# Dense matmuls in runs of three, carried over block and unit ends, in a hybrid decoder layer

## The chip, the cores and the metric

The kernel runs on one core of one Trainium2 chip. The metric is the device time of one execution in microseconds (us); the median of several runs is compared. All of the layer's weights, about 280 MB in 32-bit floats, are read once from HBM in every execution.

## The reference

One decoder layer over 256 tokens of width 2048, and a last normalization:

```
h = rms_norm(x, ln1_w);  proj = h @ w_in              # 2048 -> 10792 columns
o_a = nsa_attention(...)                              # 8 heads of 128, from proj
o_b = gated_deltanet(...)                             # 8 heads of 128, from proj
g_a, g_b = split(sigmoid(merge), 2)                   # merge: last 4096 columns of proj
x = x + (g_a * (o_a @ w_pa) + g_b * (o_b @ w_pb)) @ w_o
h = rms_norm(x, ln2_w)
x = x + square(relu(h @ w_up)) @ w_down               # 2048 -> 8192 -> 2048
out = rms_norm(x, ln_f_w)
```

The attention and the delta rule are small here; nearly all of the work is the product of 256 tokens with the weight matrices.

## The kernel before

**Tiling.** The tokens stand in the columns and the features in the partitions. A *unit* is 128 output features with a contraction over 2048, so 128 x 2048 weights. It is worked in four *blocks* (q = 0 to 3), each with four 128x128 pieces of weights. Each 32-bit operand is split into a high part that TensorE takes in its fast 32-bit format, and the low rest. The split of weights gives `wh` and `wl` (tile `wt`), that of activations 256 columns of high parts with 256 columns of low parts behind them. The product is then wh x high, wh x low and wl x high. wh meets all 512 columns in one matmul; wl meets 256 columns in another. Both add into one PSUM tile `gp` of 512 columns (three such buffers), the first with high and low products side by side; the evacuation adds the halves.

**The order of a block.** `mm3` issues a block's four 512-column matmuls (line 247; an *H* below) and then its four 256-column ones (line 249; an *l*). An H and the l of the same weights are a *pair*, so a block is four pairs, HHHH llll. Each matmul loads its own 128x128 weights, and that load runs beside the matmul before it. The first units of the kernel, which need only 256 of the columns, go by `mm3n` instead: three 256-column matmuls for each piece of weights (lines 255 to 257).

**The list of units.** `seq` sets the order: the input projections with attention and delta-rule preparation between them; 32 merge units (two for each of 16 `dm`), of which the first two end at unit nM; 16 units that project the heads (`pu`, operand `osp`, each with two halves of two blocks); at unit nB, 16 units of the output projection (`wo`, operand `m`); at nB + 16 the first half of the MLP's up-projection (32 units, operand `xs2`, which the trace calls `xs`), at nB + 48 its down-projection (32 units, operands `hA` and `hB`), at nB + 80 and nB + 112 the same for the other half. The last two units go by `mm3n`.

**The loop.** One pass of the loop at the end of `build` is one block `b`. It issues weight loads on SyncE's queue, starts the evacuations of units that ended in the block before (`pend`), splits the weights of block b + 6 (`split_at(b + LOOK)`: one ScalarE copy, line 69, and one VectorE subtraction, line 108, into one of seven `wt` buffers), issues block b's matmuls, and lets each pending small task (`step_tasks`) go on by one step. These tasks issue the attention's and the delta rule's small matmuls, *side work* below, into PSUM tiles from `sideps`; so side work stands between blocks.

Of the kernel before, what the change touches and what calls it, by code (L numbers as in the profile page):

```python
# [26 lines left out]
T = 256  # L27
# [7 lines left out]
LOOK = 6  # L35
# [13 lines left out]
def build(tc, xt, lnv, vecs, rel, onehot, win, wsm, wc, wpab, wo, wup, wdn, out):  # L49
    nc = tc.nc  # L50
    ctx = ExitStack()
    V, S, G, PE = nc.vector, nc.scalar, nc.gpsimd, nc.tensor
# [5 lines left out]
    hold = ctx.enter_context(tc.tile_pool(name="hold", bufs=1))  # L58
    psum = ctx.enter_context(tc.tile_pool(name="psum", bufs=1, space=bass.MemoryType.PSUM))
    ctx.enter_context(tc.manual_schedule())  # L60

    def sideps(name="sp"):
        return psum.tile([128, 512], F32, name=name, tag="side", bufs=4)

    def gps(name="gp"):
# [10 lines left out]
    def load(u, q, n=2):  # L76

        un = units[u]
        w = un.cols // 4
        if q % 2 == 0:  # L80
            raws[u, q // 2] = stream.tile([128, 2 * w], F32, name="raw", tag="raw", bufs=NRAW)
        o = (q % 2) * w
        nc.sync.dma_start(out=raws[u, q // 2][:, o:o + n * w], in_=un.src[:, q * w:(q + n) * w])
# [3 lines left out]
    def split(b):  # L87
        u, q = blocks[b]
        w = units[u].cols // 4
        raw = raws[u, q // 2]  # L90
        if units[u].prep:
            whs[b], wls[b] = raw, None
            return
        raw = raw[:, (q % 2) * w:(q % 2) * w + w]
        wt = stream.tile([128, 2 * w], FR, name="wt", tag="wt", bufs=LOOK + 1)
        c = 40 if units[u] is sm else w
        r, p = raw.rearrange("p (k c) -> p k c", c=c), wt.rearrange("p (k a c) -> p k a c", a=2, c=c)
        whs[b], wls[b] = (wt, None) if c < w else (wt[:, :w], wt[:, w:])
        if c < w:
            act(p[:, :, 0], r, AF.Copy)  # L100
            V.tensor_tensor(p[:, :, 1], r, p[:, :, 0].bitcast(F32), op=OP.subtract)
            return
        wh, wl = whs[b], wls[b]
        n = 2 if b == 0 else 1
        for i in range(n):
            c = slice(i * w // n, (i + 1) * w // n)
            act(wh[:, c], raw[:, c], AF.Copy)
            V.tensor_tensor(wl[:, c], raw[:, c], wh[:, c].bitcast(F32), op=OP.subtract)  # L108
            if b == 0:
                x_split(2 * i, 2)  # L110
# [70 lines left out]
    def warm(n):  # L181

        w = sideps("warm")
        for i in range(n):
            PE.matmul(w[:, :T], zs[:, :128], zs, start=(i == 0), stop=(i == n - 1))
# [7 lines left out]
    def row_pow(ps, power):  # L193

        col = tmp.tile([128, 2], F32, name="rc", tag="rc", bufs=2)
        for c in range(2):
            V.tensor_scalar(col[:, c:c + 1], ps[c][:, 0:1], 1.0 / D, EPS, op0=OP.mult, op1=OP.add)
        if power == -0.5:
            G.tensor_tensor(col, col, mhalf, op=OP.pow)
            yield  # L200
        else:
            V.reciprocal(col, col)
        dg = tmp.tile([128, 2, 128], F32, name="dg", tag="dg", bufs=1)
        for c in range(2):
            V.tensor_scalar(dg[:, c], ident, col[:, c:c + 1], None, op0=OP.mult)
        yield
        bc = sideps()
        PE.matmul(bc[:, :T], ones, dg.rearrange("p c t -> p (c t)"), start=True, stop=True)
        return bc

    def row_stat(sq, dst, power):
        ps = [sideps() for _ in range(2)]
        row_sum(ps, sq, True, True)
        bc = yield from row_pow(ps, power)
        act(dst, bc[:, :T], AF.Copy)
# [4 lines left out]
    def spawn(gen):  # L220
        tasks.append(gen)

    def start(gen):
        tasks.append(gen)
        advance(gen)

    def advance(g):
        try:
            next(g)
        except StopIteration:  # L230
            tasks.remove(g)
# [5 lines left out]
    def step_tasks():  # L237
        cnt["step"] += 1
        for g in list(tasks):
            advance(g)  # L240


    def mm3(ps, wh, wl, rhs, M, first, last):


        for j, r in enumerate(rhs):
            PE.matmul(ps[:M, :], wh[:, j * M:(j + 1) * M], r, start=(first and j == 0), stop=False)  # L247
        for j, r in enumerate(rhs):
            PE.matmul(ps[:M, :T], wl[:, j * M:(j + 1) * M], r[:, :T], start=False, stop=(last and j == 3))  # L249
# [68 lines left out]


    gk, gv, gz, kc = {}, {}, {}, {}  # L320
    cnt = {"pc": 0, "at": 0, "step": 0, "last": -9, "lb": 0, "pool": 0, "heads": 0}
    done = set()

    def ev_gdn(h, which):
# [638 lines left out]
    nM = len(seq)  # L963
# [8 lines left out]
    nB = len(seq)  # L972
# [13 lines left out]
    while u < len(units):  # L986
        n = 2 if units[u].prep else 1
# [4 lines left out]
    def x_split(k, n):  # L992
        for k in range(k, k + n):
            act(xs[:, k, :T], xT[:, k, :], AF.Copy, scale=ln1[:, k:k + 1])
            V.scalar_tensor_tensor(xs[:, k, T:], xT[:, k, :], ln1[:, k:k + 1], xs[:, k, :T].bitcast(F32),  # L995
                                   op0=OP.mult, op1=OP.subtract)
# [39 lines left out]
    def split_at(b):  # L1036
        if b >= len(blocks):
            return
        split(b)
        if 0 < b < 4 * NI and b % NI == 0:  # L1040
            x_split(4 * (b // NI), 4)
        for f, *args in sqat.get(b, ()):
            f(*args)
# [5 lines left out]
    def stat1():  # L1049
        V.tensor_scalar(vec[:, VEC_CONV:VEC_CONV + 96], vec[:, VEC_CONV:VEC_CONV + 96], 0.5, None, op0=OP.mult)  # L1050
        yield from row_stat(sqs, R, -0.5)
        spawn(bias_table())
        done.add("R")


    pend = []
# [4 lines left out]
    at = {x: b for b, x in enumerate(blocks)}  # L1061
    lastq = [at[u, q + 1] + (LOOK if units[u].prep else 0) for u, q in halves if units[u] is not sm]
    halves = [x for x in halves if x[0] >= NI]
    for b, (u, q) in enumerate(blocks):
        if b == 4 * nM + 1:
            while not all(("gdn", h) in done for h in range(H)):
                step_tasks()
            pools["a1"].release()
            pp["th"] = tc.alloc_tile_pool(name="thp", bufs=1, side="right")
        if b == 4 * nA:  # L1070
            while tasks:
                step_tasks()
            pool_a2.release()
            pool_b = tc.alloc_tile_pool(name="pb", bufs=1)
            mt["m"] = pool_b.tile([128, KD, 2 * T], FR, name="m", tag="m32")
        if b == 4 * nB:
            mt["xs2"] = hold.tile([128, KD, 2 * T], FR, name="xs2", tag="xs")
        if b == 4 * (nB + 16):
            hB = pool_b.tile([128, KD, 2 * T], FR, name="hB", tag="m32")
            mt["h"] = [hold.tile([128, 2 * T], FR, name="hA", tag=f"o{k}") for k in range(KD)]  # L1080
            mt["h"] += [hB[:, k, :] for k in range(KD)]
        while loaded < len(halves) and lastq[max(0, loaded + 6 - NRAW)] < b + LOOK:
            load(*halves[loaded])
            loaded += 1
        if "R" in done:
            for f, ps in pend:
                start(f(ps))
            pend = []
        if b == 4 * nB:
            pp["th"].release()  # L1090
            pool_x = tc.alloc_tile_pool(name="px", bufs=1, side="right")
            mt["x"] = pool_x.tile([128, KD, T], F32, name="x2")
            for c in range(4):
                nc.gpsimd.dma_start(out=mt["x"][:, 4 * c:4 * c + 4, :], in_=xt[:, 4 * c:4 * c + 4, :])
        split_at(b + LOOK)
        for n in (12, 20):
            if b + n < len(blocks):
                un = units[blocks[b + n][0]]
                if un.prep and blocks[b + n][1] == 0 and (un is cu[0, 0]) == (n == 20):
                    spawn(un.prep())  # L1100
        un = units[u]
        ps = un.gemm(q, whs.pop(b), wls.pop(b))
        if b == 4 * NI:
            pool_x0.release()
            pools["a1"] = tc.alloc_tile_pool(name="pa1", bufs=1)
            spawn(stat1())
        if q in un.evac:
            pend.append((un.evac[q], ps))
        clock += 0.44 if un.prep else 1.3
        if clock >= 1.2:  # L1110
            clock = 0.0
            step_tasks()
# [9 lines left out]
    y = pool_b.tile([128, 2, D], F32, name="y", tag="m32")  # L1122
# [85 lines left out]
```

## Time and profile before

| what | value |
|---|---|
| median of 3 runs | 1493.62 us (1493.16 to 1494.17) |
| profiled execution, its own time | 1492.99 us |
| span of that execution, first to last instruction | 1491.2 us |
| TensorE (PE) busy | 99% of the span, 9578 matmuls recorded |
| VectorE (DVE), ScalarE (ACT), GpSimd (POOL) busy | 70%, 55%, 17% |
| DMA | 285 MB, 191 GB/s |
| chain of work that ended last | 89% on PE, 47% on line 247, 24% on line 249 |

The span is read as one long row of matmuls with some holes. Since a matmul's record overlaps the next one's, its duration says little; what a matmul costs is the distance from its start to the start of the next one. That is called its *step* here. The timeline view merges equal matmuls that follow each other, gives the start of the first and how many there are, and so gives the steps of a run by the difference of two rows.

### The profile page before, as it was taken

What the parts mean: (1) busy time and instruction counts of PE and PEld (TensorE: products, weight loads), DVE (VectorE), ACT (ScalarE), POOL (GpSimd) and SP (SyncE); (2) the same over time, 40 slices, a digit from 0 to 9 for tenths busy, and PEclk for the clock granted to TensorE, in tenths of its full rate; (3) what the DMA queues carried; (4) which work ended last, traced back from release to release, by engine and by line L of the source; (5) the groups of instructions that cost most, each with busy time, mean ns of one, the idle gap of its engine ahead of it and who ended that gap; (6) DMA issues with size and microseconds to landing.
All of it is one profiled execution on the core that took longest, in us unless ns stands there. A gap on an engine that the chain in (4) does not pass through costs nothing.

```text
span 1491.2 us, 26400 instructions
## 1 busy us (share of the span) xinstructions
PE 1475.2 (99%) x9578; PEld 1319.6 (88%) x9578; DVE 1038.1 (70%) x2062; ACT 814.9 (55%) x1738; POOL 259.3 (17%) x615
## 2 busy tenths in 40 slices
PE   8999999999999999999999999999999999999997
PEld 7999998889988888888888888888888888888887
DVE  7877777656787677787986776665566767766664
ACT  6655565545565555565655555544445555555553
POOL 1066788742000000002320000000000000011211
PEclk9999999999999999999999999999999999999999
DMA  8466666786444555556655555555555555555552
GB/s 288 156 194 192 191 209 191 221 264 230 146 143 158 180 192 188 192 190 222 215 188 192 188 194 188 193 188 194 188 186 195 190 191 190 192 189 191 188 193 75
DMA packets 86446, 285.33 MB, mean 191 GB/s; under 512 B 13187, under 2 KB 14723, under 8 KB 86316
## 3 DMA queue, kind: packets, MB, share of 16 engines
q1 hardware_dynamic: 85596, 281.52, 57.9%
q0 software_dynamic: 576, 2.10, 0.4%
q8 instruction: 75, 1.23, 0.3%
q14 instruction: 55, 0.45, 0.1%
q10 hardware_dynamic: 144, 0.02, 0.0%
HBM read 279.20 MB, written 4.41 MB: 190 GB/s over the span
## 4 chain that ended last, share of the span: by engine, by line
PE 89%; issue 3%; POOL 2%; DVE 2%; DMA 2%; ACT 1%; SPq 0%; POOLq 0%; DVEq 0%; ACTq 0%
PE gp L247 47%; PE gp L249 24%; PE gp L255 5%; PE gp L256 4%; PE gp L257 4%; DMA raw<-in_win_dram 1%; DMA ldr<-lq 1%; POOL ft L492 1%; PE cps L644 1%; POOL tb L494 1%; ACT wt L69 1%; PE pAo L788 0%; DVE wt L108 0%; PE pPT L777 0%; PE pK L453 0%
## 5 line engine op out<-in xcount | busy, mean ns | idle before, releaser
L108 DVE TENSOR_TENSOR wt<-raw,wt 128x512 fp32r<-128x512 f32 (+1 forms) x977 | 682.9, 706 | 328.7 <-ACT wt L69 322.4
L69 ACT ACTIVATE wt<-raw 128x512 fp32r<-128x512 f32 (+1 forms) x977 | 604.0, 625 | 301.9 <-PE gp L249 159.2
L247 PE MATMUL gp<-xs,wt 128*128 128x512 f32 x1536 | 419.5, 395 | 0.0
L247 PEld LDWEIGHTS gp<-xs,wt 128*128 128x128 f32 x1536 | 261.2, 188 | 33.4
L249 PEld LDWEIGHTS gp<-xs,wt 128*128 128x128 f32 x1536 | 232.8, 188 | 32.3
L255 PE MATMUL gp<-xs,wt 128*128 128x256 f32 x832 | 244.7, 294 | 1.5 <-ACT xs L69 0.9
L249 PE MATMUL gp<-xs,wt 128*128 128x256 f32 x1536 | 239.7, 278 | 0.0
L257 PE MATMUL gp<-xs,wt 128*128 128x256 f32 x832 | 232.7, 280 | 0.3 <-DVE wt L108 0.2
L256 PE MATMUL gp<-xs,wt 128*128 128x256 f32 x832 | 232.8, 280 | 0.1
L255 PEld LDWEIGHTS gp<-xs,wt 128*128 128x128 f32 x832 | 156.6, 188 | 11.4 <-issue 5.8
L256 PEld LDWEIGHTS gp<-xs,wt 128*128 128x128 f32 x832 | 156.8, 188 | 1.1 <-DVE xs L995 0.7
L257 PEld LDWEIGHTS gp<-xs,wt 128*128 128x128 f32 x832 | 156.3, 188 | 1.1 <-DVE wt L108 1.1
L247 PE MATMUL gp<-hA,wt 128*128 128x512 f32 x496 | 134.4, 393 | 0.0
L247 PE MATMUL gp<-hB,wt 128*128 128x512 f32 x496 | 134.4, 393 | 0.0
L69 ACT ACTIVATE a<-gp 128x256 f32<-128x256 f32 x175 | 67.1, 383 | 105.8 <-PE gp L249 105.6
L290 DVE TENSOR_TENSOR t<-gp,a 128x256 f32<-128x256 f32 x159 | 67.5, 425 | 56.1 <-ACT a L69 56.0
L918 POOL TENSOR_TENSOR sqs<-x 128x256 f32<-128x256 f32 x1 | 0.9, 906 | 541.8 <-DVE x L905 541.8
L494 POOL TENSOR_TENSOR tb<-tb,ft 128x62 f32<-128x62 f32 (+30 forms) x248 | 90.4, 365 | 19.4
L247 PEld LDWEIGHTS gp<-hB,wt 128*128 128x128 f32 x496 | 84.2, 188 | 10.6
L247 PEld LDWEIGHTS gp<-hA,wt 128*128 128x128 f32 x496 | 84.2, 188 | 10.7
L249 PEld LDWEIGHTS gp<-hA,wt 128*128 128x128 f32 x496 | 75.2, 188 | 10.4
L249 PEld LDWEIGHTS gp<-hB,wt 128*128 128x128 f32 x496 | 75.2, 188 | 10.4
(278 smaller groups left out, 1555.4 us busy)
## 6 DMA issues: line engine op xcount, KB each, us to landing
raw<-in_win_dram SPq DMA_DIRECT2D x162, 512.0 KB, 4.4
raw<-in_wup_dram SPq DMA_DIRECT2D x128, 512.0 KB, 4.4
raw<-in_wdn_dram SPq DMA_DIRECT2D x128, 512.0 KB, 4.4
raw<-in_wpab_dram SPq DMA_DIRECT2D x32, 512.0 KB, 4.4
raw<-in_wo_dram SPq DMA_DIRECT2D x32, 512.0 KB, 4.2
raw<-in_wc_dram SPq DMA_DIRECT2D x16, 512.0 KB, 5.7
lb<-ldr SPq DMA_DIRECT2D x32, 128.0 KB, 5.2
raw<-in_win_dram SPq DMA_DIRECT2D x11, 256.0 KB, 7.8
```

Source lines behind the costliest of these rows:

```text
L69: return S.activation(o, i, f, **kw)
L108: V.tensor_tensor(wl[:, c], raw[:, c], wh[:, c].bitcast(F32), op=OP.subtract)
L247: PE.matmul(ps[:M, :], wh[:, j * M:(j + 1) * M], r, start=(first and j == 0), stop=False)
L249: PE.matmul(ps[:M, :T], wl[:, j * M:(j + 1) * M], r[:, :T], start=False, stop=(last and j == 3))
L255: PE.matmul(ps[:M, :T], w, r[:, :T], start=(first and j == 0), stop=False)
L256: PE.matmul(ps[:M, :T], w, r[:, T:], start=False, stop=False)
L257: PE.matmul(ps[:M, :T], wl[:, j * M:(j + 1) * M], r[:, :T], start=False, stop=(last and j == 3))
L290: V.tensor_tensor(t[:M], ps[:M, :T], a[:M], op=OP.add)
L492: G.tensor_tensor(ft[:, :, :w], tb[:, :, j:j + 1].to_broadcast([128, 2, w]), lbs[j // 16][:, j - o, :, j - o + 1:], op=OP.mult)
L494: G.tensor_tensor(tb[:, :, j + 1:], tb[:, :, j + 1:], ft[:, :, :w], op=OP.subtract)
L644: PE.matmul(ps[32 * j:32 * j + 32, :256], sf[:, 2 * q - 2 + j, :], wh[:, 256 * j:256 * j + 256], start=(u == 0 and q == 1), stop=(u == 3 a ...
L918: G.tensor_tensor(sqs, x2, x2, op=OP.mult)
```

## The change

From the merge units' third one on (block 4 nM), `mm3` keeps the l matmuls in a list, `run["lo"]`, and issues them after every third H (`run["need"]`), whatever block or unit these H belong to. So the order is HHH lll, and a run goes over block and unit ends. After side work (a counter in `sideps` tells of it) the next run counts four H; l that were kept before the side work are issued with it, five or six in a row. At the units in `ends` (nB, nB + 16, nB + 48, nB + 80, nB + 112 and the last two) the kept l are issued at the end of the block, and the next run has four H.

```diff
+    run = {"on": False, "side": 0, "n": 0, "need": 3, "lo": []}
+
+    def run_flush(need):
+        for p, M, w, r, stop in run["lo"]:
+            PE.matmul(p[:M, :T], w, r[:, :T], start=False, stop=stop)
+        run.update(n=0, need=need, lo=[])
...
     def mm3(ps, wh, wl, rhs, M, first, last):
+        if run["on"]:
+            if run["side"] != cnt["side"]:
+                run.update(side=cnt["side"], n=0, need=4)
+            for j, r in enumerate(rhs):
+                PE.matmul(ps[:M, :], wh[:, j * M:(j + 1) * M], r, start=(first and j == 0), stop=False)
+                run["lo"].append((ps, M, wl[:, j * M:(j + 1) * M], r, last and j == 3))
+                run["n"] += 1
+                if run["n"] == run["need"]:
+                    run_flush(3)
+            return
...
+    ends = [4 * x - 1 for x in (nB, nB + 16, nB + 48, nB + 80, nB + 112, nB + 142, nB + 144)]
     for b, (u, q) in enumerate(blocks):
+        if b == 4 * nM:
+            run["on"] = True
...
         if "R" in done:
+            late = [x for x in pend if any(x[1] is y[0] for y in run["lo"])]
             for f, ps in pend:
-                start(f(ps))
-            pend = []
+                if not any(ps is y[1] for y in late):
+                    start(f(ps))
+            pend = late
...
-        split_at(b + LOOK)
+        if not run["on"]:
+            split_at(b + LOOK)
...
         ps = un.gemm(q, whs.pop(b), wls.pop(b))
+        if b in ends:
+            run_flush(4)
+        if run["on"]:
+            split_at(b + LOOK)
```

Two things come with it. A unit whose last l are still kept has its evacuation started one block later (`late`). And the split of block b + 6 is issued behind block b's matmuls, since the `wt` buffer that it takes is that of block b - 1, whose last l may stand among them.

The matmuls' number and operands stay as they were: 3040 pairs by `mm3` in both programs. The three places that matter follow, on PE's queue; line 261 is where the changed `mm3` issues an H, and line 249 is by chance an l in both.

The first place is the last side work of the attention (`pAo`) among the merge and head projections. Before:

```order
L247 MATMUL gp<-xs,wt 128x512 x4
L249 MATMUL gp<-xs,wt 128x256 x4
L786 MATMUL pAo<-pt,vcp 128x256
L788 MATMUL pAo<-pt,vall 128x256
L789 MATMUL pAo<-pt,vall 128x128
L788 MATMUL pAo<-pt,vall 128x256
L789 MATMUL pAo<-pt,vall 128x128
L247 MATMUL gp<-xs,wt 128x512 x4
L249 MATMUL gp<-xs,wt 128x256 x4
L247 MATMUL gp<-xs,wt 128x512 x4
```

And with the change:

```order
L261 MATMUL gp<-xs,wt 128x512 x2
L806 MATMUL pAo<-pt,vcp 128x256
L808 MATMUL pAo<-pt,vall 128x256
L809 MATMUL pAo<-pt,vall 128x128
L808 MATMUL pAo<-pt,vall 128x256
L809 MATMUL pAo<-pt,vall 128x128
L261 MATMUL gp<-xs,wt 128x512 x4
L249 MATMUL gp<-xs,wt 128x256 x6
L261 MATMUL gp<-xs,wt 128x512 x3
L249 MATMUL gp<-xs,wt 128x256 x3
```

Two H go ahead of the side work, their l go behind it with four others, and then 178 runs of three follow up to the end of the head projections, where two H are left over.

The second place is the step from the first up-projection (operand `xs_9062`, that is `xs2`) to its down-projection (`hA`). Before:

```order
L247 MATMUL gp<-xs_9062,wt 128x512 x4
L249 MATMUL gp<-xs_9062,wt 128x256 x4
L247 MATMUL gp<-hA,wt 128x512 x4
L249 MATMUL gp<-hA,wt 128x256 x4
L247 MATMUL gp<-hA,wt 128x512 x4
```

And with the change:

```order
L261 MATMUL gp<-xs_9062,wt 128x512 x3
L249 MATMUL gp<-xs_9062,wt 128x256 x3
L261 MATMUL gp<-hA,wt 128x512 x4
L249 MATMUL gp<-hA,wt 128x256 x4
L261 MATMUL gp<-hA,wt 128x512 x3
```

Here the count comes out even, no H is left over, and a single run of four stands between runs of three.

The third place is the step from that down-projection (`hB`) to the second up-projection. Before:

```order
L247 MATMUL gp<-hB,wt 128x512 x4
L249 MATMUL gp<-hB,wt 128x256 x4
L247 MATMUL gp<-xs_9062,wt 128x512 x4
L249 MATMUL gp<-xs_9062,wt 128x256 x4
L247 MATMUL gp<-xs_9062,wt 128x512 x4
```

And with the change:

```order
L249 MATMUL gp<-hB,wt 128x256 x3
L261 MATMUL gp<-hB,wt 128x512
L249 MATMUL gp<-hB,wt 128x256
L261 MATMUL gp<-xs_9062,wt 128x512 x4
L249 MATMUL gp<-xs_9062,wt 128x256 x4
L261 MATMUL gp<-xs_9062,wt 128x512 x3
```

One H is left over, so a run of one goes ahead of the run of four. The step from the second up-projection to its down-projection looks the same.

## Rows read from the trace of the kernel before

**Rows 1.** The page's first part, busy time by engine, and the granted clock.

```profile
PE 1475.2 (99%) x9578; PEld 1319.6 (88%) x9578; DVE 1038.1 (70%) x2062; ACT 814.9 (55%) x1738; POOL 259.3 (17%) x615
...
PEclk9999999999999999999999999999999999999999
```

**Rows 2.** Busy time by stretch: length, then each engine's busy time and count, clock.

```profile
500.00:770.00 270.00, 270.00 (x1563) 236.82 (x1562) 209.27 (x372) 155.46 (x310) 28.57 (x33) 1.00 0.60 198
780.00:1465.00 685.00, 685.00 (x3962) 600.82 (x3961) 450.87 (x775) 363.32 (x666) 27.73 (x27) 1.00 0.57 189
```

**Rows 3.** Timeline of PE in a steady stretch: start us, us, instruction, count.

```profile
900.14 1.09 PE L247 MATMUL gp<-xs,wt 128*128 128x512 f32 x4
901.07 0.62 PE L249 MATMUL gp<-xs,wt 128*128 128x256 f32 x4
901.52 1.07 PE L247 MATMUL gp<-xs,wt 128*128 128x512 f32 x4
902.43 0.63 PE L249 MATMUL gp<-xs,wt 128*128 128x256 f32 x4
902.90 1.09 PE L247 MATMUL gp<-xs,wt 128*128 128x512 f32 x4
...
1453.47 1.09 PE L247 MATMUL gp<-hB,wt 128*128 128x512 f32 x4
```

**Rows 4.** The same timeline, cut so that a run's fourth H stands alone.

```profile
900.84 0.39 PE L247 MATMUL gp<-xs,wt 128*128 128x512 f32 x1
...
902.21 0.39 PE L247 MATMUL gp<-xs,wt 128*128 128x512 f32 x1
```

**Rows 5.** Timeline of PE in the first part, ends of two rows of 256-column matmuls.

```profile
19.57 0.28 PE L255 MATMUL gp<-xs,wt 128*128 128x256 f32 x1
...
23.65 0.39 PE L279 MATMUL sp<-xs,wt 128*80 128x512 f32 x1
...
65.32 0.28 PE L256 MATMUL gp<-xs,wt 128*128 128x256 f32 x1
...
90.29 0.38 PE L429 MATMUL pT<-ident,oraw 128*128 128x128 f32 x2
```

**Rows 6.** Timeline of PE behind side work of the attention (lines 777 to 789).

```profile
487.92 0.27 PE L778 MATMUL pPT<-ident,pc 128*128 128x128 f32 x1
487.94 1.16 PE L247 MATMUL gp<-xs,wt 128*128 128x512 f32 x4
488.94 0.62 PE L249 MATMUL gp<-xs,wt 128*128 128x256 f32 x4
489.40 1.07 PE L247 MATMUL gp<-xs,wt 128*128 128x512 f32 x4
...
493.82 1.18 PE L247 MATMUL gp<-xs,wt 128*128 128x512 f32 x4
494.84 0.62 PE L249 MATMUL gp<-xs,wt 128*128 128x256 f32 x4
495.29 0.39 PE L247 MATMUL gp<-xs,wt 128*128 128x512 f32 x1
```

**Rows 7.** Timeline of PE behind other side work, where the long l run follows.

```profile
469.11 1.27 PE L247 MATMUL gp<-xs,wt 128*128 128x512 f32 x4
470.22 0.63 PE L249 MATMUL gp<-xs,wt 128*128 128x256 f32 x4
470.69 1.09 PE L247 MATMUL gp<-xs,wt 128*128 128x512 f32 x4
...
775.41 1.28 PE L247 MATMUL gp<-xs,wt 128*128 128x512 f32 x4
776.54 0.63 PE L249 MATMUL gp<-xs,wt 128*128 128x256 f32 x4
777.01 1.09 PE L247 MATMUL gp<-xs,wt 128*128 128x512 f32 x4
777.93 0.63 PE L249 MATMUL gp<-xs,wt 128*128 128x256 f32 x4
778.40 1.09 PE L247 MATMUL gp<-xs,wt 128*128 128x512 f32 x4
```

**Rows 8.** Waits of ACT, 780 to 1465 us: us in total, times, longest.

```profile
ACT wt L69 <- PE gp L249: 126.1, 187, 0.8
ACT a L69 <- PE gp L249: 66.1, 93, 0.8
```

More of the change, by code (lines that the diff above doesn't have):

```diff
@@ L60, in build @@
     ctx.enter_context(tc.manual_schedule())
+    cnt = {"pc": 0, "at": 0, "step": 0, "last": -9, "lb": 0, "pool": 0, "heads": 0, "side": 0}
     def sideps(name="sp"):
+        cnt["side"] += 1
         return psum.tile([128, 512], F32, name=name, tag="side", bufs=4)
@@ L320, in build @@
     gk, gv, gz, kc = {}, {}, {}, {}
-    cnt = {"pc": 0, "at": 0, "step": 0, "last": -9, "lb": 0, "pool": 0, "heads": 0}
     done = set()
```

## Prediction

> **What bounds the kernel now.** I read the busy shares and the clock first. TensorE is busy for 99% of the span, and its granted clock is 9 or more tenths in every slice, so it stands at the upper of its two levels, 2.4 GHz, throughout [rows 1]. Then the stretches: between 500 and 770 us and between 780 and 1465 us PE has no hole at all, while ScalarE, VectorE and GpSimd are far from full [rows 2]. So past the first part only the distance between PE's own starts counts, and I read that from the timeline.
>
> In the steady stretch a block takes 1.38 us. From 900.14 to 1453.47 us there are 400 blocks without any side work, so one takes 553.33 / 400 = 1.3833 us, and a pair 345.8 ns [rows 3]. But two forms of block take turns. In form A (start 900.14) the four H take 0.93 us and the four l 0.45; in form B (start 901.52) 0.91 and 0.47 [rows 3]. So an l is not of one length. The first part shows its two lengths better: 36 steps in a row of 256 columns between 19.57 and 23.65 us make 113.3 ns each, and 212 in a row between 65.32 and 90.29 us make 117.8 [rows 5]. Nothing else changes within such a row, so a matmul's step depends on a state that the matmuls before it leave behind, and that state can stay. I call a run of l at 113.3 short and one at 117.8 long.
>
> What sets the state can be read from the steady blocks. Form B begins behind short l; its first three H take 0.69 us (901.52 to 902.21), its fourth 0.22, and then the l are long [rows 3, 4]. Form A begins behind long l; three H take 0.70 (900.14 to 900.84), the fourth 0.23, and the l are short [rows 3, 4]. Four H always turn one kind into the other.
>
> **Part 1: runs of three in place of four.** What do l do behind three H that began on short l? The steady rows don't show it, but the places behind side work do: there the first H step is long, three common ones follow, and then l. At 487.94 the four H take 1.00 us, of which 0.31 is the first, and the l behind them are short (488.94 to 489.40, 0.46, which is 454 ns); at 493.82 it is 1.02 and 0.45 [rows 6]. These three H are of the lengths that open form B. So my reading is that the H go through a cycle of three steps, and three H that begin on short l end where l are short again: HHH lll repeats itself. Its cost: form B's H run is 1383.3 - 4 x 117.8 = 912 ns, less a fourth step between 220 and 230, so three H are 682 to 692; with three short l (340) the triple is 1022 to 1032, so 340.7 to 344.0 ns a pair. I take the middle, 342.3, a gain of 3.5 ns a pair (bounds 1.8 to 5.1).
>
> The other order that can hold itself is the one entered on long l: form A's three H (0.70 us, so 695 to 705 ns) and then l that stay long (3 x 117.8 = 353) make 1048 to 1058, so 349 to 353 ns a pair. I take 351.1, a loss of 5.3 (bounds 3.5 to 6.9). Thus the change is no gain in itself: each stretch falls into one of two orders, 3.5 ns below or 5.3 ns above today's mean, and keeps it until something breaks the run.
>
> **Part 2: what sets the order of each stretch.** From the program's order I count the pairs of each stretch, and what stands at its start.
> - Merge units with attention's side work (216 pairs): some 96 of them go in threes, each group behind a run of four after side work. Of 27 places behind side work in this trace 22 have short l (two of them in [rows 6], the other kind in [rows 7]). Gain 0.3 us.
> - From the last attention head to nB (540 pairs): behind `pAo`. All seven such places in the trace lead to short l, as at 493.82 [rows 6]. Gain 540 x 3.5 = 1.9 us.
> - Output projection (264 pairs): behind two left-over H, two l and a run of four. No row shows runs of two; it may come out on either order, 0.9 us less or 1.4 more. I take nothing.
> - First up-projection (494 pairs): behind the row statistics' side work, where today the l are long (776.54 to 777.01, 0.47), then four H take 0.92 us, and the l are long once more (777.93 to 778.40) [rows 7]. If the last of these four H is the one that leads from short to long, as in form B, then three would end on short, and I take the gain, 1.7 us. The other end is a loss of 2.6.
> - First down-projection (512 pairs): here a run of four stands alone between threes. By form B, four H that begin on short l end on long ones, and the threes behind them then stay long: a loss of 512 x 5.3 = 2.7 us.
> - Second up-projection (512) and second down-projection (480 pairs): behind one left-over H, one l and a run of four. One H and one l shift the state by a step, which no row shows from the long order; if it ends as four H from long l do in form A, the l are short. I take the gain, 1.8 and 1.7 us; the other end is a loss of 2.7 and 2.5.
>
> Sum: -0.3 - 1.9 + 0 - 1.7 + 2.7 - 1.8 - 1.7 = -4.7 us.
>
> **Part 3: what is moved with it.** The split of block b + 6 is issued behind block b's matmuls, and waits for l that may go up to one triple (1.03 us) later. On ScalarE's queue the evacuation copies stand behind it, and VectorE's subtraction follows from it. ScalarE already waits for PE at this place, 187 times with 0.8 us at most [rows 8]: the weights are split as early as a buffer comes free, six blocks (8.3 us) ahead of their use, and 1.03 us of that is hidden. If that cover were gone, each block would show a hole. The evacuation of a unit whose l are kept starts a block (1.38 us) later; the next unit but two needs its PSUM buffer, at the narrowest place (the last head projections, a buffer for two blocks) 4 blocks or 5.5 us after the end, against a copy and two additions. I cost both at nothing. No DMA is added, and the loads keep their place on SyncE's queue. What is late next is still PE.
>
> The profiled execution's own time is 1492.99 us, 0.6 below the median of the runs, 1493.62. The sum is made in its steps; 1492.99 - 4.7 = 1488.3, and against the median 1488.9, which I take.
>
> **The rivals.** *All stretches short.* If the run of four at the first down-projection doesn't turn the order, and the output projection falls well, the gains are 0.3 + 1.9 + 0.9 + 1.7 + 1.8 + 1.8 + 1.7 = 10.1 us: 1483.5. Against it stands form B, where four H from short l end on long l at every one of some 350 blocks. Chance 0.15.
>
> *Long order kept to the end (slower).* If one H and one l don't bring the long order back, the first down-projection, the second up-projection and the second down-projection all stay long: -0.3 - 1.9 + 0 - 1.7 + 2.7 + 2.7 + 2.5 = +4.0, so 1497.6. It decides as soon as two of the three big stretches behind nB + 48 are long. For it: the same left-over of one stands at both ends, so what fails once fails twice, and today long l appear behind side work too [rows 7]. Chance 0.27.
>
> *Nothing gained or lost.* Both forms of block sum to 1.38 us although their parts differ [rows 3]; a fixed supply behind PE would do that, and regrouping would leave 1383.3 ns for every four pairs: 1493.6. Against it: 36 short steps in a row are never paid back [rows 5], and behind side work common H and short l stand together (1.46 us less the 0.08 by which the first step is longer is the same 1.38, though, so it is not excluded) [rows 6]. Chance 0.10. [...]
>
> **How the numbers follow.** The mixed forecast, 1488.9, has 0.48; with its bounds (1.8 to 5.1 and 3.5 to 6.9 a pair, the output projection either way) it is 1486.5 to 1491.5. With the rivals: all short 0.15, nothing 0.10, long to the end 0.27. About 0.2% (3.0 us) is what a measurement of this kernel can tell from no change. Faster by more than that: 0.15 and nearly all of the forecast, 0.60. Within it: nothing, and the edges of the others, 0.14. Slower: 0.26. The range must reach from near the all-short case to the long one, 1483.5 to 1497.8; the forecast's own range stands above.
>
> **What would show it.** In the profile after, threes of l of 0.34 us with H runs of 0.69 are the short order, 0.35 with 0.70 the long one. The stretch from the last `pAo` to the output projection should be short, about 1.9 us less than before; the first down-projection long; the second up-projection tells the forecast from its rival. I am wrong if l runs of both lengths still take turns within a stretch, if PE shows holes behind the splits, or if a stretch changes its order without side work or a run of four.

## The result: slower by half a per cent

The changed kernel takes 1501.03 us (median of 6 runs, 1499.94 to 1503.39) against 1493.65 us before: ratio 1.0052, 95% interval 1.0041 to 1.0062. The forecast was 1488.9, and the slower rival 1497.6; the time lies 3.4 us beyond that too. The profiled execution took 1503.39 us, the slowest of the six, with a span of 1501.5 us against 1491.2.

The page of the profile after says as little as that of before [rows 1]: PE is busy for 99% at the full granted clock, and has no hole where it had none.

```profile
PE 1483.9 (99%) x9578; PEld 1325.5 (88%) x9578; DVE 1029.7 (69%) x2062; ACT 824.9 (55%) x1738; POOL 258.8 (17%) x615
...
PEclk9999999999999999999999999999999999999999
```

So again the steps of PE tell it. In the timeline of the kernel after (start us, us, instruction, count), line 261 is an H and line 249 an l. Three stretches, each with its first H and l and the H of its last triple:

```profile
497.61 0.85 PE L261 MATMUL gp<-xs,wt 128*128 128x512 f32 x3
498.30 0.52 PE L249 MATMUL gp<-xs,wt 128*128 128x256 f32 x3
...
681.69 0.85 PE L261 MATMUL gp<-osp,wt 128*128 128x512 f32 x3
...
684.80 0.86 PE L261 MATMUL gp<-m,wt 128*128 128x512 f32 x3
685.50 0.52 PE L249 MATMUL gp<-m,wt 128*128 128x256 f32 x3
...
772.23 0.86 PE L261 MATMUL gp<-m,wt 128*128 128x512 f32 x3
...
782.13 0.85 PE L261 MATMUL gp<-xs,wt 128*128 128x512 f32 x3
782.82 0.50 PE L249 MATMUL gp<-xs,wt 128*128 128x256 f32 x3
...
948.45 0.85 PE L261 MATMUL gp<-xs,wt 128*128 128x512 f32 x3
```

Here are three orders, not two. From 782.13 to 948.45 us 162 triples take 1.0267 us each, 342.2 ns a pair: H 0.69, l 0.34, the *short* order. From 684.80 to 772.23 us 83 triples take 1.0534, 351.1 ns a pair: H 0.70, l 0.36, the *long* order. And from 497.61 to 681.69 us 177 triples take 1.0400, 346.7 ns a pair: H 0.69 as in the short order, but l of 0.35. This *middle* order was not in the prediction. Within a stretch an order never changes; the alternation of the blocks before [rows 3] is gone.

Read from start to start in the trace, the three H steps of the short order are 226, 229 and 232 ns, those of the middle one 229, 232 and 226, and those of the long one 233, 236 and 229. So the middle order has the short one's three H, begun a step later. In the eight kernels of this study that load all weights, the l go with the last H ahead of them: behind a step of 231 or 232 ns they are short, behind any other they are long, in 7476 of 7487 cases. Why that is so is not shown. Within each of these three stretches every step keeps its length to 1 ns, so no wait for a split or a buffer stands among them.

The places where it changes are those with side work or a run of another length. Behind the even end at 949.48 and behind the left-over pair at 1128.88:

```profile
949.48 1.07 PE L261 MATMUL gp<-hA,wt 128*128 128x512 f32 x4
950.39 0.63 PE L249 MATMUL gp<-hA,wt 128*128 128x256 f32 x4
950.86 0.86 PE L261 MATMUL gp<-hA,wt 128*128 128x512 f32 x3
...
1128.88 0.40 PE L261 MATMUL gp<-hB,wt 128*128 128x512 f32 x1
1129.11 0.28 PE L249 MATMUL gp<-hB,wt 128*128 128x256 f32 x1
1129.23 1.09 PE L261 MATMUL gp<-xs,wt 128*128 128x512 f32 x4
1130.16 0.63 PE L249 MATMUL gp<-xs,wt 128*128 128x256 f32 x4
1130.63 0.86 PE L261 MATMUL gp<-xs,wt 128*128 128x512 f32 x3
```

The run of four at 949.48 begins on short l and is form B (0.91 and 0.47); the threes behind it are long. At 1128.88 the order goes in long and comes out long (0.93, then l of 0.47). The stretches add up as follows, by the first matmul of each, in the kernel before and then in the one after:

```profile
385.46 1.18 PE L247 MATMUL gp<-xs,wt 128*128 128x512 f32 x4
680.65 1.07 PE L247 MATMUL gp<-m,wt 128*128 128x512 f32 x4
769.19 1.07 PE L247 MATMUL gp<-xs,wt 128*128 128x512 f32 x4
947.17 1.09 PE L247 MATMUL gp<-hA,wt 128*128 128x512 f32 x4
1124.24 1.09 PE L247 MATMUL gp<-xs,wt 128*128 128x512 f32 x4
1301.30 1.09 PE L247 MATMUL gp<-hA,wt 128*128 128x512 f32 x4
1467.30 0.28 PE L255 MATMUL gp<-hA,wt 128*128 128x256 f32 x1
```

```profile
387.84 1.18 PE L268 MATMUL gp<-xs,wt 128*128 128x512 f32 x4
683.42 1.07 PE L261 MATMUL gp<-m,wt 128*128 128x512 f32 x4
773.28 1.09 PE L261 MATMUL gp<-xs,wt 128*128 128x512 f32 x4
1309.00 1.09 PE L261 MATMUL gp<-hA,wt 128*128 128x512 f32 x4
1477.53 0.28 PE L276 MATMUL gp<-hA,wt 128*128 128x256 f32 x1
```

| stretch | before, us | after, us | difference | order of the threes |
|---|---|---|---|---|
| merges and head projections | 295.19 | 295.58 | +0.39 | middle, from 497.61 on |
| output projection | 88.54 | 89.86 | +1.32 | long |
| first up-projection | 177.98 | 176.20 | -1.78 | short |
| first down-projection | 177.07 | 179.75 | +2.68 | long |
| second up-projection | 177.06 | 179.77 | +2.71 | long |
| second down-projection, 30 units | 166.00 | 168.53 | +2.53 | long |

Together +7.85 us, which agrees with the medians' +7.4. The other 2.4 us by which the two spans differ lie ahead of 387.84 us, where both programs have the same order; that start lay between 385.0 and 387.8 us in the profiles of this study, whichever kernel it was.

### The profile page after: what moved, and what is told of

It is laid out like the page before. It is cut to its first block, busy times and chain, and to the rows that moved or that the text cites. A ratio compares the mean times of both kernels' runs of the same rounds, so it can differ in the third digit from the quotient of the medians.

```text
span 1501.5 us, 26421 instructions
## 1 busy us (share of the span) xinstructions
PE 1483.9 (99%) x9578; PEld 1325.5 (88%) x9578; DVE 1029.7 (69%) x2062; ACT 824.9 (55%) x1738; POOL 258.8 (17%) x615
## 4 chain that ended last, share of the span: by engine, by line
PE 88%; issue 4%; DVE 2%; POOL 2%; DMA 2%; ACT 1%; SPq 1%; POOLq 0%; DVEq 0%; ACTq 0%
PE gp L261 46%; PE gp L249 23%; PE gp L276 4%; PE gp L277 4%; PE gp L278 4%; DMA raw<-in_win_dram 1%; ACT wt L71 1%; DVE wt L110 1%; POOL ft L512 1%; POOL tb L514 1%; PE gp L268 0%; PE pAo L808 0%; PE cps L664 0%; SPq L492 0%; DMA tskew<-big 0%
## 5 line engine op out<-in xcount | busy, mean ns | idle before, releaser
L261 PE MATMUL gp<-xs,wt 128*128 128x512 f32 x1504 | 430.8, 395 | 0.0
L249 PE MATMUL gp<-xs,wt 128*128 128x256 f32 x1504 | 254.0, 278 | 0.0
L276 PE MATMUL gp<-xs,wt 128*128 128x256 f32 x832 | 245.5, 295 | 1.7 <-ACT wt L71 1.7
L278 PE MATMUL gp<-xs,wt 128*128 128x256 f32 x832 | 233.3, 280 | 0.6 <-DVE wt L110 0.4
L277 PE MATMUL gp<-xs,wt 128*128 128x256 f32 x832 | 233.1, 280 | 0.1
L261 PE MATMUL gp<-hB,wt 128*128 128x512 f32 x496 | 145.7, 395 | 0.0
L261 PE MATMUL gp<-hA,wt 128*128 128x512 f32 x496 | 145.4, 395 | 0.0
L249 PEld LDWEIGHTS gp<-hB,wt 128*128 128x128 f32 x496 | 82.5, 188 | 14.8
L249 PEld LDWEIGHTS gp<-hA,wt 128*128 128x128 f32 x496 | 82.4, 188 | 14.8
L261 PEld LDWEIGHTS gp<-hA,wt 128*128 128x128 f32 x496 | 82.4, 188 | 7.6
L261 PEld LDWEIGHTS gp<-hB,wt 128*128 128x128 f32 x496 | 82.4, 188 | 7.5
L249 PE MATMUL gp<-hB,wt 128*128 128x256 f32 x496 | 88.8, 281 | 0.0
L249 PE MATMUL gp<-hA,wt 128*128 128x256 f32 x496 | 88.4, 281 | 0.0
```

What stands on the lines that cost most here:

```text
L249: PE.matmul(p[:M, :T], w, r[:, :T], start=False, stop=stop)
L276: PE.matmul(ps[:M, :T], w, r[:, :T], start=(first and j == 0), stop=False)
L277: PE.matmul(ps[:M, :T], w, r[:, T:], start=False, stop=False)
```

## Experiments

Theory: the order alone costs or saves the time. A stretch of threes holds the order that it was entered in, and a run of another length moves it to another one. Rival: the bookkeeping costs it, that is the splits issued behind the matmuls and the evacuations that start a block later. The rival has something in the profile: ScalarE's waits for PE at the split rose from 126.1 us in 187 pieces [rows 8] to 265.2 in 398. PE itself shows no wait in the profile after between 395 and 1480 us.

```profile
ACT wt L71 <- PE gp L249: 265.2, 398, 1.3
```

All ratios below are to the kernel before, with 95% intervals.

### The change with fours

```diff
-                if run["n"] == run["need"]:
-                    run_flush(3)
+                if run["n"] == run["need"]:
+                    run_flush(4)
```

> The changed kernel with runs of four everywhere: PE's order is that of the kernel before, but the split of weights stands behind the block's matmuls. Order theory: 1493.6 as before, forms A and B taking turns. Rival (the later split costs): slower than 1493.6, up to the 1501 of the changed kernel.

1493.68 us, ratio 1.0001 (0.9992 to 1.0009). With PE's order as before, the later split is free. ScalarE waits for PE there because it is early, and that cover was deep enough. With a block as a run no evacuation starts late here; that part of the rival stands until the last experiments.

### Three in place of four where nothing is left over

```diff
         if b in ends:
-            run_flush(4)
+            run_flush(4 if run["lo"] else 3)
```

> The changed kernel, except that where no H is left over at a unit end (nB + 16, nB + 48) the next run has three H and not four. Order theory: a stretch of threes holds one of three orders (342.2, 346.7 or 351.1 ns a pair) until a run of another length moves it; without the run of four the first down-projection stays at 342.2, and behind H2 l2 H4 l4 at nB + 80 the second up-projection and, behind H1 l1 H4 l4, the second down-projection too: about 13 us less than the changed kernel, some 1488. Rival (the change's bookkeeping costs: splits issued later, evacuations a block later): nothing of that is altered, so 1501.

1487.19 us, ratio 0.9950 (0.9938 to 0.9962), 13.8 us less than the changed kernel. The first down-projection in its timeline, from its first matmul to the next stretch's first:

```profile
948.31 0.85 PE L261 MATMUL gp<-hA,wt 128*128 128x512 f32 x3
...
1123.53 1.08 PE L261 MATMUL gp<-xs,wt 128*128 128x512 f32 x4
```

It takes 175.22 us in place of 179.75, and the two stretches behind it take 175.25 and 164.29 in place of 179.77 and 168.53, together 13.3 us less. One run of three for one of four at the start sets 1500 pairs, since the order stays. The head projections stayed middle (346.7 ns a pair) and the output projection long (89.87 us): nothing was altered ahead of them.

### One run of four more, in the middle of a long stretch

```diff
+        if b == 4 * (nB + 64) - 1:
+            run["more"] = True
...
                 if run["n"] == run["need"]:
-                    run_flush(3)
+                    run_flush(4 if run.pop("more", False) else 3)
```

> The changed kernel with one single run of four in the middle of the first down-projection, where threes take 351.1 ns a pair. Order theory: that one run turns the order, so the second half goes at 342.2 (256 pairs by 8.9 = 2.3 us less), and the run of four at nB + 80, where now nothing is left over, turns it back: 1498.7. Rival: one run in 250 changes nothing, 1501, and no change of pace at that place.

1497.18 us, ratio 1.0023 (1.0014 to 1.0032). The place, and the ends of the stretch around it:

```profile
943.68 1.07 PE L261 MATMUL gp<-hA,wt 128*128 128x512 f32 x4
...
1034.60 1.09 PE L261 MATMUL gp<-hA,wt 128*128 128x512 f32 x4
...
1035.98 0.85 PE L261 MATMUL gp<-hA,wt 128*128 128x512 f32 x3
...
1121.19 1.07 PE L261 MATMUL gp<-xs,wt 128*128 128x512 f32 x4
```

Ahead of 1034.60 a triple takes 1.053 us, behind 1035.98 it takes 1.027, up to the end of the stretch: from 1035.98 to 1121.19 there are 83 triples. The stretch takes 177.51 us, 2.24 less than in the changed kernel, where 2.3 was expected, and the run of four at 1121.19, which begins on short l, makes the next one long again (179.76). So one run changes the pace of the next 250 pairs or more, either way. In this execution the head projections were in the short order and the output projection too (293.11 and 87.64 us in place of 295.58 and 89.86), although the program up to there is the same as the changed kernel's. That is 4.7 us, more than the run of four saves, so what this run is worth is read from its stretch and not from the ratio. The places behind the attention's side work thus don't fall alike in every execution. This fits the wide spread of the three kernels that run threes among side work (3.5, 5.0 and 6.1 us, against 2.1 with fours); that their runs differ by this was not seen, and one of the 23 runs of the kernel before lay 2.7 us above its others too.

### A version that keeps the short order everywhere

Fours while side work goes on, one run of four to enter, threes from there, and left-overs made up at the end of a stretch by two runs of two or two of four, so that a stretch ends in the order in which it began:

```diff
-            if run["side"] != cnt["side"]:
-                run.update(side=cnt["side"], n=0, need=4)
...
+    def next_need():
+        if run["left"] == 4:
+            return 4 if run["need"] == 4 else 2
+        return {8: 4, 2: 2}.get(run["left"], 3)
...
+        if b == 4 * (nB + 16):
+            run["on"] = False
+        if not run["on"] and 4 * nM <= b < 4 * (nB + 142) and ready(b):
+            run.update(on=True, need=4, left=4 * (min(x for x in ends if x >= b) + 1 - b))
...
-        if b in ends:
-            run_flush(4)
+        if b in ends and run["on"]:
+            run.update(need=3, left=4 * min([x - b for x in ends if x > b] + [999]))
```

Here `ready` is true when all attention heads, or the row statistics, are done.

> Threes from the block behind the last side work on, entered by one run of four; fours (as before) while side work goes on and around the row statistics; the left-over made up at a stretch's end by two runs of two or two of four, so that nothing is left over and no single run of four stands between threes. Order theory: every stretch at 342.2 ns a pair; 2,780 pairs by 3.6 = 10 us less than before, 1483.7. Rival (bookkeeping): slower than 1493.6. The two runs of two at the end of the output projection are the part that no row has shown; if they land elsewhere, the stretch behind goes at 346.7 or 351.1 until the side work there.

1483.82 us, ratio 0.9931 (0.9920 to 0.9943), as expected to 0.1 us, and better than both kernels. Its stretches begin at:

```profile
678.80 0.85 PE L269 MATMUL gp<-m,wt 128*128 128x512 f32 x3
...
766.42 1.07 PE L277 MATMUL gp<-xs,wt 128*128 128x512 f32 x4
...
942.63 0.85 PE L269 MATMUL gp<-hA,wt 128*128 128x512 f32 x3
...
1117.88 0.85 PE L269 MATMUL gp<-xs,wt 128*128 128x512 f32 x3
...
1293.12 0.85 PE L269 MATMUL gp<-hA,wt 128*128 128x512 f32 x3
```

87.62, 176.21, 175.25 and 175.24 us against 88.54, 177.98, 177.07 and 177.06 before: all four are short, and so is the last (164.27 against 166.00). Evacuations here start late just as in the changed kernel, so they cost nothing either, and the rival is out.

### Other lengths of run

Both are the planned version with another number in place of three; with six, weights are split five blocks ahead.

```diff
-        return {8: 4, 2: 2}.get(run["left"], 3)
+        return {8: 4, 2: 2}.get(run["left"], 6)
```

> The planned version with runs of six in place of three (left-overs by two runs of two or of four; weights split five blocks ahead in place of six, with the same number of buffers). Order theory: H go through a cycle of three, so six H that begin on short l end on short l too; all l short, 342.2 ns a pair, 1483.8 like the planned threes. Rival (what helps is that runs are shorter than a block): slower than the threes, towards 1493.6 or above.

1483.46 us, ratio 0.9933 (0.9918 to 0.9948), the same as with threes. Six H take 1.37 us, the steps of 226, 229 and 232 ns twice, and six l 0.68, all of them short:

```profile
601.74 1.53 PE L269 MATMUL gp<-osp,wt 128*128 128x512 f32 x6
603.11 0.84 PE L259 MATMUL gp<-osp,wt 128*128 128x256 f32 x6
603.79 1.54 PE L269 MATMUL gp<-osp,wt 128*128 128x512 f32 x6
```

> The planned version with runs of two everywhere (one run of four at each entry). Order theory, from the steps seen so far: two runs of two make a cycle, the first with H of 226 and 229 and l of 120 and 118, the second with H of 229 and 232 and two short l: 1380 ns for four pairs, 345.0 a pair, and every other order leads into it; 2,780 pairs by 0.8 less than before, 1491.3. Rival (shorter runs help as such): below the 1483.8 of the threes.

1490.82 us, ratio 0.9982 (0.9972 to 0.9991), 0.5 us from the 1491.3 expected. Two forms take turns, 1.38 us for four pairs. The one that begins at 600.48 has H of 0.46 and short l of 0.23, the other H of 0.45 and longer l of 0.24:

```profile
600.48 0.62 PE L267 MATMUL gp<-xs,wt 128*128 128x512 f32 x2
600.94 0.39 PE L257 MATMUL gp<-xs,wt 128*128 128x256 f32 x2
601.17 0.62 PE L267 MATMUL gp<-xs,wt 128*128 128x512 f32 x2
601.62 0.40 PE L257 MATMUL gp<-xs,wt 128*128 128x256 f32 x2
601.86 0.62 PE L267 MATMUL gp<-xs,wt 128*128 128x512 f32 x2
```

So neither a run shorter than a block nor a longer one helps as such: three and six are good because H go through a cycle of three.

### Halved weights, to see what makes a step long

An H steps at 226 to 236 ns here and an l at 113 to 120. The load of the next matmul's weights goes on beside it, and it was my guess for what makes a step long. Two variants of the kernel before load 64 in place of 128 columns of weights, in the H or in the l. In their profiles such a load takes 134 ns in place of 188; the matmul then writes 64 partitions in place of 128.

```diff
+            n = M if first and j == 0 else M // 2
-            PE.matmul(ps[:M, :], wh[:, j * M:(j + 1) * M], r, start=(first and j == 0), stop=False)
+            PE.matmul(ps[:n, :], wh[:, j * M:j * M + n], r, start=(first and j == 0), stop=False)
```

> The kernel before, with only 64 of the 128 weight columns in the 512-column matmuls by mm3 but for the first of each unit: half of the high weights' product is left out. If the load of the next weights makes the step longer: the first three steps of an H run fall from 226 to 236 towards 216, the last step of an l run falls to near 109, the other l steps stay at 113 or 118. Rival (the step belongs to the matmul itself): all steps stay.

One execution, 1480.28 us. The H steps did not fall towards 216: they are 226, 229, 232 and 227 ns, as in form B. But the l behind them are short now, where form B has long ones, and away from side work every block takes 1.37 us:

```profile
1000.85 1.07 PE L248 MATMUL gp<-hB,wt 128*64 128x512 f32 x4
1001.76 0.62 PE L250 MATMUL gp<-hB,wt 128*128 128x256 f32 x4
1002.21 1.08 PE L248 MATMUL gp<-hB,wt 128*64 128x512 f32 x4
```

The other variant does the same to the l (`n = M if last and j == 3 else M // 2`):

> The kernel before, with only 64 of the 128 weight columns in the 256-column matmuls by mm3 but for the last of each unit: half of the low weights' product is left out. With halved weights in the 512-column matmuls the H steps kept their length (226 to 232), so a step's surplus over its columns is not the time of the load beside it; what changed was which order held, all l short. If so here too, l steps stay at 113 or 118 and H steps at 226 to 236, with the forms of block in another turn or only one of them. If the load beside an l did set its two lengths, the first three l steps of a run fall to near 109.

One execution, 1505.73 us: with less to load it is slower. The l did not fall to 109. The H run takes 0.93 us as in form A, but the l behind it, short there, are long here (0.47, steps of 115 to 120 ns), and away from side work every block takes 1.40 us:

```profile
1001.26 1.09 PE L247 MATMUL gp<-hA,wt 128*128 128x512 f32 x4
1002.19 0.63 PE L250 MATMUL gp<-hA,wt 128*64 128x256 f32 x4
1002.66 1.09 PE L247 MATMUL gp<-hA,wt 128*128 128x512 f32 x4
```

So the guess fell: a shorter load did not shorten the step that it goes on beside. What the halving moved is which l follow the same H. Whether the shorter load does that, or the fewer partitions written, was not separated, and what makes a step long stays open.

## Why the prediction was wrong

**Right.** PE's steps, not another engine, set the time. Step lengths depend on a state that the matmuls before leave behind. Three H that begin on short l end on short l; the short order's cost (342.3 forecast, 342.2 measured) and the long one's (351.1 and 351.1) were read from the steady blocks and from the places behind side work. That they fit to 0.1 ns is luck, since the bounds were 340.7 to 344.0 and 349 to 353. The first up-projection came out short (-1.7 forecast, -1.78), which had been a guess between two ends; the first down-projection long (+2.7 and +2.68), as form B said; and what is moved with the change cost nothing, as the fours and the planned version showed.

**Wrong: which order each stretch would have.** Three terms of the sum failed, all at entries that the kernel before doesn't have, and I took the good end at two of them.
- *Second up- and down-projection*, taken as -1.8 and -1.7, came to +2.71 and +2.53, the bad end of the bounds (+2.7 and +2.5). The step that failed is that one left-over H and l would shift the long order so that four H end on short l: behind them four H of 0.93 us were followed by l of 0.47 (1129.23), so "four H always turn one kind into the other", read from the steady blocks, doesn't hold behind such an entry. The kernel with three at the even end shows the other half: entered in the short order, the same left-over of one and the run of four come out short. So that pair of runs keeps either order, and what went wrong at nB + 48 stayed to the end, as the slower rival had it.
- *Last attention head to nB*, taken as -1.9 (and -0.3 for the pieces ahead), came to +0.39 for both. Two things failed here. Behind `pAo` all places of before led to short l [rows 6] (eight with the first one, at 392.18 us; the prediction counts seven), and I took that to hold for the new entry too, with two H ahead of the side work and their l behind it. But what comes behind the new entry depends on the order in which it is reached. At 467.04 us in the profile after, the threes ahead of the side work are short, the six l behind it take 0.68 us (468.05 to 468.73), and short threes follow. At 495.89 the threes ahead are long, the six l take 0.71 (496.90 to 497.61), and the middle order follows. The six l agree with the threes ahead at all 18 such places of the three profiles that have this entry, 13 short and five long; and the long order came from other side work some 15 us earlier, where the same program went on in the short order in the kernel with one more four. And the order that came was the middle one, which I didn't know of: behind long l I had seen only the H of form A (0.70 us for three), and took it that no others could stand there; in the middle order three H of 0.69 us do.

```profile
468.05 0.84 PE L249 MATMUL gp<-xs,wt 128*128 128x256 f32 x6
468.73 0.85 PE L261 MATMUL gp<-xs,wt 128*128 128x512 f32 x3
...
496.90 0.87 PE L249 MATMUL gp<-xs,wt 128*128 128x256 f32 x6
```

- *Output projection*, taken as 0, came to +1.32, the bad end (+1.4): behind the middle order the two left-over H and the run of four lead to the long one. Behind the short order, as in the kernel with one more four, they lead to the short one.

With the orders that came, the prediction's own prices, with 0.9 ns for each of 536 pairs in the middle order and the pieces ahead at nothing, give +0.5 + 1.4 - 1.7 + 2.7 + 2.7 + 2.5 = +8.1 us, against +7.85 measured. So the mechanism was right but for the third order, and the state at the entries was guessed where it had to be known. The range was also too narrow for its own bounds: with 1.8 to 5.1 ns gained on 2,122 pairs, 3.5 to 6.9 lost on 512, and the output projection either way, the mixed forecast reaches from 1483.7 to 1494.7, not only from 1486.5 to 1491.5. The measured time is outside both.

**The rivals.** The all-short case is real and was reached by the planned version (1483.8, forecast for it 1483.5), but not by this change. The slower rival's condition came true, all three stretches behind nB + 48 being long; its 1497.6 lacks what the head and output projections cost. *Nothing gained or lost* is out: three orders with the same matmuls differ by 8.9 ns a pair. The Trainium skill ("TensorE: Matmul & The Clock Gate", section "Back-to-back issue gap") gives columns / 2.4 + 2.5 ns as the gap of an isolated matmul at the upper clock; an estimate from that is 325 ns for a pair. Here the same two shapes take 342.2, 346.7 or 351.1 ns.

## What to carry to other kernels

When PE is never idle at the full clock, read the distances between matmul starts run by run: an equal mean can hide two step lengths, and which one comes can depend on how many matmuls of each shape stand in a row. What a regrouping is worth that can lock into a good or a bad order can't be told until each entry is known, so plan the run lengths at the ends and behind side work, so that a stretch hands on the order in which it came. A single run of another length is a cheap experiment: if one group of matmuls changes the pace of the next 250 pairs, whose own work is unchanged, the pace hangs on a state that the group left behind.

## What the runs showed of the hardware

- Matmuls of one shape, back to back on an engine that shows no wait, keep one of several step lengths over hundreds of matmuls: 113.3 or 117.8 ns for 256 columns, and 342.2, 346.7 or 351.1 ns for a pair in threes.
- The state outlives changes of operand, of PSUM buffer and of unit, and a single run of four 512-column matmuls among threes moves it (351.1 to 342.2 ns a pair, and back).
- Behind a 512-column matmul that steps at 231 or 232 ns the 256-column ones are short, behind one of another step long, in 7476 of 7487 cases. With halved weights this no longer holds.
- Halving the weight columns of the 512-column matmuls made the l steps short away from side work (blocks of 1.37 us); halving those of the 256-column ones made them long (1.40 us), so that the kernel became slower with less to load (1505.73 us, one execution).
- Behind side work the same program can fall into different orders in different executions: 295.58 and 293.11 us for the same first stretch.
